# A second, rounding transfer for the high parts of weights in the mixer

## The chip, the cores and the metric

The kernel runs on one core of a Trainium2 chip. The metric is the device time of one launch in microseconds, the median of three runs. The profile shows one execution of the same program.

## What is computed

The reference is two decoder layers on 512 tokens of 1024 channels, all in float32:

```python
for l in range(DEPTH):                       # DEPTH = 2
    x = layer_norm(ALPHA * x + 0.5 * swiglu(x, ffn1_wg[l], ffn1_wu[l], ffn1_wd[l]), ...)
    x = layer_norm(ALPHA * x + token_mixer(x, w_in[l], ...), ...)
    x = layer_norm(ALPHA * x + 0.5 * swiglu(x, ffn2_wg[l], ffn2_wu[l], ffn2_wd[l]), ...)
# token_mixer: x @ w_in gives queries, latents, keys, values, and two gates of 1024 channels;
#   o_m = 8 heads of latent attention; o_n = 8 heads of sparse attention (compressed, selected, window)
#   y = sigmoid(gate_m) * (o_m @ w_proj_mla) + sigmoid(gate_n) * (o_n @ w_proj_nsa);  return y @ w_out
```

## The kernel before

**Products.** A float32 product is made of three matmuls in the type fp32r (`mm3`, lines 226 to 229): each operand is split into a high part, which is the value rounded to fp32r, and a low part, which is the value minus the high part. The three are high by high, high by low and low by high.

**The stream of weights.** All weights lie in DRAM in the order of use (`full_plan`), cut into chunks of at most 128x1024 (512 KB). The class `Stream` (from line 241) brings them in. `load` issues one transfer per chunk from SyncE (SP) into a ring of three tiles `raw` (`RAW_RING`). `pump` splits a chunk: ScalarE (ACT) writes the high part (line 301), VectorE (DVE) the low part (`sub_lo`, line 224), both into one tile `hl` of a ring of four (`HI_RING`); a `raw` tile is free again when both have read it, and an `hl` tile when TensorE (PE) has done the last matmul with it. The program calls `pump` in `get` (a chunk is fetched) and in `done` (a chunk is used up); there it splits chunks up to `LOOK` = 2 beyond those fetched. `live` counts the `hl` tiles in use.

**The mixer.** The attention part of a layer is written as a list of some 200 named steps, `SCHEDULE`. `S`, `N`, `T`, `P` with a number are the scores and softmax, the normalising, the transposing and the product with the values of one of 24 attention units. Between them stand steps that use weights: `m4a` to `m7b` and `n0a` to `n7b` (gates of the two branches, a chunk each, half of it in each of two steps), `cw00` to `cw11` (the compression's first matrix, four chunks), `p0` to `p7` (the first branch's output projection, a chunk for every two), `c2` (192 columns). `keys` and `v0` to `v3` hold four chunks each; `v3` releases the last four one after another. `w_proj_nsa` and `w_out` follow behind the list.

**Other transfers of the mixer.** GpSimd (POOL) issues stores and loads of intermediates: `sv` (values, line 998), `sg` (gates, line 729), `gl` (gates back, line 903), `sy` (results, line 897), `ym` and `tn` (lines 1304 and 1305). SP issues `lc` (line 1023, the step `cl1`), which reads back the values that `sv` stored; the transposes of the step `cb1` (`cd`, line 1040) need them.

**What sets the order.** The program runs under a planner that orders the instructions of PE, ACT, DVE and SP by the order of the text and by when it thinks their inputs are ready, on a model of its own. So a conversion may be placed ahead of the step that calls for it, as soon as its `hl` tile is free. POOL is taken out of this (`manual_schedule`): its instructions stand in the order of the text, and each waits for its own inputs with the next ones behind it. Every engine works through its list in order.

Of the kernel before, what the change touches and what calls it, by code (L numbers as in the profile page):

```python
# [12 lines left out]
AF = mybir.ActivationFunctionType  # L13
# [30 lines left out]
PEND_AT = 3  # L44
TAIL = 4
GROUPS = (10, 8)
LOOK_PAIR = 4

PASS, STAY, TAIL_KIND, PAIR_A, PAIR_B, PAIR_C = range(6)

# [29 lines left out]
def stat_chunk(name, l, c0):  # L82
    return [(name, l, k, c0, c0 + 128) for k in range(KB)]


def tok_chunks(l, c0, c1):
    return [[("w_in", l, 2 * c + j, c0, c1) for j in range(2)] for c in range(KB // 2)]


def uq_chunk(l, half):  # L90
    return [("w_uq", l, k, half * 384, half * 384 + 384) for k in range(2)]


def ukv_chunk(l, part):
    return [("w_ukv", l, 0, part * 512, part * 512 + 512)]


def w1_chunk(l, kind, jh):
    return [("cmp_k_w1" if kind == 0 else "cmp_v_w1", l, 8 * jh + j, 0, 128) for j in range(8)]


def w2_chunk(l):
    return [("cmp_k_w2", l, 0, 0, 64), ("cmp_k_w2", l, 0, 0, 64), ("cmp_v_w2", l, 0, 0, 64)]


def proj_chunk(l, name, m):
    return [(name, l, k, c * 128, c * 128 + 128) for c in (m, m + 1) for k in range(4)]


def down_chunk(name, l, dh, i):  # L110
    return [(name, l, 2 * i + j, dh * 512, dh * 512 + 512) for j in range(2)]


def pair_chunk(name, l, p, part):

    k, halves = ((2 * p, (0, 1)), (2 * p + 1, (1,)), (2 * p + 1, (0, 1)))[part]
    return [(name, l, k, dh * 512, dh * 512 + 512) for dh in halves]


def gate_chunk(l, which, m):  # L120
    return stat_chunk("w_in", l, (COL_GM if which == "m" else COL_GN) + m * 128)


def layer_plan(l):


    p = []

    def add(c, kind=PASS):
        p.append((c, kind))  # L130

    def down(name, nkb):
        n = nkb // 2
        for dh in range(2):
            for i in range(n):
                add(down_chunk(name, l, dh, i), TAIL_KIND if dh == 1 and i >= n - TAIL else PASS)

    def tok(c0, c1):
        for c in tok_chunks(l, c0, c1):
            add(c)  # L140

    def ffn(n):
        at = 0
        for g in GROUPS + (0,):
            end = at + g if g else NF
            for fi in range(at, end):
                add(stat_chunk(n + "_wg", l, fi * 128))
                add(stat_chunk(n + "_wu", l, fi * 128))
            pairs = range(at // 2, end // 2)
            at = end  # L150
            if g:
                for j in pairs:
                    add(pair_chunk(n + "_wd", l, j, 0), PAIR_A)
                    add(pair_chunk(n + "_wd", l, j, 1), PAIR_B)
                for j in pairs:
                    add(pair_chunk(n + "_wd", l, j, 2), PAIR_C)
            else:
                for j in pairs:
                    for dh in range(2):
                        add(down_chunk(n + "_wd", l, dh, j), TAIL_KIND)  # L160

    ffn("ffn1")
    for m in range(4):
        add(gate_chunk(l, "m", m))
    tok(COL_A, COL_B)
    tok(COL_B, COL_C)
    add(uq_chunk(l, 0))
    add(uq_chunk(l, 1))
    add(ukv_chunk(l, 0), STAY)
    add(ukv_chunk(l, 1))  # L170
    for n in SCHEDULE:
        if n == "keys":
            tok(COL_C, COL_D)
        elif n == "v0":
            tok(COL_D, COL_GM)
        elif n[0] in "mn" and n[-1] == "a":
            add(gate_chunk(l, n[0], int(n[1])))
        elif n[:2] == "cw":
            add(w1_chunk(l, int(n[2]), int(n[3])))
        elif n == "c2":  # L180
            add(w2_chunk(l))
        elif n[0] == "p" and n[1] in "0246":
            add(proj_chunk(l, "w_proj_mla", int(n[1])))
    for m in range(0, KB, 2):
        add(proj_chunk(l, "w_proj_nsa", m))
    down("w_out", KB)
    ffn("ffn2")
    return p


def full_plan():
    return [c for l in range(L) for c in layer_plan(l)]


def width(chunk):
    return sum(c[4] - c[3] for c in chunk)
# [3 lines left out]
def hybrid_kernel(ctx: ExitStack, tc: tile.TileContext, x, wflat, lnp, rmsg, small, cst, out):  # L200
    nc = tc.nc
# [7 lines left out]
    def slab(name, dt=F32):  # L209
        return slabs.tile([128, 512], dt, tag="slab", name=name)  # L210
# [9 lines left out]
    act = nc.scalar.activation  # L220
    mm = nc.tensor.matmul

    def sub_lo(o, src, hi):
        tt(out=o, in0=src, in1=f(hi), op=ALU.subtract)  # L224
# [6 lines left out]
    class Chunk:  # L231
        def __init__(self, hi, lo, w, both):
            self.hi, self.lo, self.w, self.both = hi, lo, w, both
# [7 lines left out]
    class Stream:  # L241


        def __init__(self):
            self.plan = full_plan()
            self.n_dma = self.n_split = self.n_got = self.live = 0
            self.off = 0
            self.raw = {}
            self.parts = {}
            self.sums = []  # L250

# [3 lines left out]
        def load(self, most=RAW_RING):  # L255
            while self.n_dma < len(self.plan) and self.n_dma < self.n_split + most:
                i = self.n_dma
                n = width(self.plan[i][0])
                t = rings.tile([128, 1024], F32, tag="raw", bufs=RAW_RING, name=f"raw{i}")
                src = wflat[self.off:self.off + 128 * n].rearrange("(p n) -> p n", p=128)  # L260
                step = self.piece(i, n)
                for j in range(0, n, step):
                    nc.sync.dma_start(out=t[:, j:min(n, j + step)], in_=src[:, j:min(n, j + step)])
                self.off += 128 * n
                self.raw[i] = t
                self.n_dma += 1

        def pump(self):
            self.load()
            while self.n_split < self.n_dma:  # L270
                i = self.n_split
                chunk, kind = self.plan[i]
                look = LOOK
                if kind == TAIL_KIND:
                    look = LOOK_TAIL
                elif kind >= PAIR_A:
                    look = LOOK_PAIR
                elif self.n_got and self.plan[self.n_got - 1][1] == TAIL_KIND:
                    look = LOOK_HEAD
                if i >= self.n_got + look or (kind not in (STAY, TAIL_KIND) and self.live >= HI_RING):  # L280
                    break
                n = width(chunk)
                if kind >= PAIR_A:
                    self.pair(i, kind)
                    continue
                if kind != PASS:
                    w = 512
                    hi = [slab(f"whi{i}", F32R) for _ in range(0, n, w)]
                    lo = [slab(f"wlo{i}", F32R) for _ in range(0, n, w)]
                else:  # L290
                    w = 1024
                    t = rings.tile([128, 2, w], F32R, tag="hl", bufs=HI_RING, name=f"hl{i}")
                    hi, lo = [t[:, 0, :]], [t[:, 1, :]]
                    self.live += 1
                r = self.raw.pop(i)
                step = min(w, self.piece(i, n))
                for j in range(0, n, step):
                    e = min(step, n - j)
                    a = j % w
                    h = hi[j // w][:, a:a + e]  # L300
                    act(out=h, in_=r[:, j:j + e], func=AF.Copy)  # L301
                    sub_lo(lo[j // w][:, a:a + e], r[:, j:j + e], h)
                self.parts[i] = Chunk(hi, lo, w, t if kind == PASS else None)
                self.n_split += 1
                self.load()

# [244 lines left out]
    def ffn(l, n, ln_idx, last):  # L551
# [19 lines left out]
        done = 0  # L571
        for g in GROUPS:
            ops = []
# [888 lines left out]
```

## Time and profile before

| what | value |
|---|---|
| median of three runs | 2219.08 us (2218.5 to 2219.31) |
| the profiled execution | 2218.88 us |
| its span, from the first to the last instruction | 2217.1 us |
| granted TensorE clock, mean | 0.999 of 2.4 GHz |
| mixer steps with weights, layer 1 and layer 2 | about 486 to 700 us and 1586 to 1800 us of the span |
| DMA, mean over the span | 118 GB/s |
| transfers issued by POOL | 34.61 MB, 4.4% of the 16 DMA engines' time |

The profile gives the busy time of each engine, by stretch and by line, and for each idle stretch of an engine what ended it. A line such as 224 or 301 belongs to a helper that many places call; the tile's name tells which place it is (`hl` is a streamed weight, `pl` the low part of attention weights). PE is TensorE's matmuls, PEld its weight loads. POOL's DMA instructions are the issue on the engine, and the time to landing runs from there to the last byte's arrival.

### The profile page before, as it was taken

The numbers are of one execution on the slowest core, as the hardware profiler recorded it, in microseconds if no ns is written. First come the engines' busy times: TensorE is split into PE (matmuls) and PEld (weight loads), VectorE is DVE, ScalarE is ACT, GpSimd is POOL, SyncE is SP. The second block draws the span as 40 slices with busy tenths as digits, with TensorE's granted clock in tenths as the row PEclk, the third lists the DMA queues.
The fourth block names the chain that finished last, engine by engine and source line by source line (L and its number), as shares of the span: only waits on it lengthen the run. The fifth ranks groups of instructions, "written<-read, shape, count | busy, mean of one in ns | idle before, by whom it ended". The sixth has DMA issues, their size and how long they took to land. (4 is left out here: it accounts for less than half of the span.)

```text
span 2217.1 us, 29650 instructions
## 1 busy us (share of the span) xinstructions
PE 2195.5 (99%) x11138; PEld 1880.9 (85%) x11138; DVE 1521.7 (69%) x2886; ACT 965.8 (44%) x1810; POOL 102.9 (5%) x166
## 2 busy tenths in 40 slices
PE   9999999999999999999999999999999999999998
PEld 8888889998888888888898888899988889888886
DVE  5585676578887656758655948665788966576586
ACT  3343332469765233334333434314797742343331
POOL 0000001010002000000000000010100010000000
PEclk9999999999999999999999999999999999999999
DMA  5333343344225233424422433433432272333242
GB/s 177 91 122 115 100 146 121 119 137 131 98 84 205 95 105 92 141 86 133 132 73 89 141 102 105 155 115 110 139 130 91 72 247 69 103 110 123 81 138 86
DMA packets 91520, 261.03 MB, mean 118 GB/s; under 512 B 18801, under 2 KB 22001, under 8 KB 91377
## 3 DMA queue, kind: packets, MB, share of 16 engines
q1 hardware_dynamic: 80464, 224.01, 31.6%
q0 software_dynamic: 10624, 34.61, 4.4%
q8 instruction: 87, 1.43, 0.3%
q10 hardware_dynamic: 288, 0.52, 0.1%
q14 instruction: 57, 0.46, 0.1%
HBM read 234.99 MB, written 24.12 MB: 117 GB/s over the span
## 5 line engine op out<-in xcount | busy, mean ns | idle before, releaser
L224 DVE TENSOR_TENSOR hl<-raw,hl 128x1024 fp32r<-128x1024 f32 (+5 forms) x391 | 443.4, 1140 | 208.7 <-ACT hl L301 163.0
L301 ACT ACTIVATE hl<-raw 128x1024 fp32r<-128x1024 f32 (+2 forms) x283 | 288.8, 1022 | 485.0 <-issue 214.2
L227 PE MATMUL gu<-xTh,hl 128*128 128x512 f32 x1280 | 498.0, 389 | 0.0
L228 PE MATMUL gu<-xTl,hl 128*128 128x512 f32 x1280 | 498.0, 389 | 0.0
L229 PE MATMUL gu<-xTh,hl 128*128 128x512 f32 x1280 | 497.9, 389 | 0.0
L227 PEld LDWEIGHTS gu<-xTh,hl 128*128 128x128 f32 x1280 | 240.3, 188 | 49.9
L228 PEld LDWEIGHTS gu<-xTl,hl 128*128 128x128 f32 x1280 | 240.3, 188 | 49.7
L229 PEld LDWEIGHTS gu<-xTh,hl 128*128 128x128 f32 x1280 | 240.3, 188 | 49.7
L556 DVE TENSOR_TENSOR t<-t,gu 128x512 f32<-128x512 f32 x80 | 55.0, 688 | 174.2 <-PE gu L229 174.2
L310 ACT ACTIVATE hl<-raw 128x1024 fp32r<-128x1024 f32 (+1 forms) x108 | 97.4, 916 | 124.3 <-PE gu L229 85.3
L555 DVE SCALAR_TENSOR_TENSOR t<-t,gu 128x512 f32<-128x512 f32 x80 | 54.9, 686 | 140.3 <-ACT t L554 140.3
L554 ACT ACTIVATE t<-gu 128x512 f32<-128x512 f32 x80 | 47.5, 594 | 205.3 <-PE gu L229 205.3
L680 ACT ACTIVATE P<-P,nm 128x384 f32<-128x384 f32 x192 | 105.6, 552 | 39.0 <-DVE nm L678 34.8
L227 PE MATMUL d<-hl,ph_s 128*128 128x512 f32 x288 | 113.0, 392 | 1.1 <-DVE u L530 0.9
L228 PE MATMUL d<-hl,ph_s 128*128 128x512 f32 x288 | 112.1, 389 | 0.0
L229 PE MATMUL d<-hl,pl_s 128*128 128x512 f32 x288 | 112.1, 389 | 0.0
L224 DVE TENSOR_TENSOR pl<-pt,ph 128x512 fp32r<-128x512 f32 x144 | 79.2, 595 | 23.8 <-ACT ph L704 23.3
L426 POOL TENSOR_TENSOR rs<-rs,ct 128x1 f32<-128x1 f32 x24 | 22.3, 930 | 1515.5 <-DVE rs L425 1515.5
L382 ACT ACTIVATE xTh<-xtp 128x512 fp32r<-128x512 f32 x48 | 25.6, 598 | 147.1 <-PE xtp L379 147.1
L678 DVE CUSTOM_DVE_ANT_0 P<-sc,maskw 128x384 f32<-128x384 f32 x192 | 82.8, 485 | 2.3 <-PE sc L672 2.1
L227 PE MATMUL gf<-xTh,hl 128*128 128x512 f32 x192 | 77.2, 402 | 0.0
L229 PE MATMUL gf<-xTh,hl 128*128 128x512 f32 x192 | 75.2, 392 | 0.0
(366 smaller groups left out, 4603.2 us busy)
## 6 DMA issues: line engine op xcount, KB each, us to landing
raw<-in_wflat_dram SPq DMA_DIRECT2D x343, 512.0 KB, 3.5
raw<-in_wflat_dram SPq DMA_DIRECT2D x40, 256.0 KB, 2.6
gb<-in_lnp_dram SPq DMA_DIRECT2D x24, 256.0 KB, 5.7
raw<-in_wflat_dram SPq DMA_DIRECT2D x12, 384.0 KB, 3.1
sy<-gl POOLq DMA_DIRECT2D x16, 256.0 KB, 2.8
xr<-spill SPq DMA_DIRECT2D x16, 256.0 KB, 5.6
ym<-sy POOLq DMA_DIRECT2D x16, 256.0 KB, 6.3
raw<-in_wflat_dram SPq DMA_DIRECT2D x8, 416.0 KB, 4.0
```

Of the source, the lines that this page charges most:

```text
L224: tt(out=o, in0=src, in1=f(hi), op=ALU.subtract)
L227: mm(o, lh, rh, start=start, stop=False)
L228: mm(o, lh, rl, start=False, stop=False)
L229: mm(o, ll, rh, start=False, stop=stop)
L301: act(out=h, in_=r[:, j:j + e], func=AF.Copy)
L310: act(out=hi, in_=r, func=AF.Copy)
L382: act(out=h, in_=bv, func=AF.Copy)
L554: act(out=t, in_=g, func=AF.Tanh, scale=0.5)
L555: stt(out=t, in0=t, scalar=1.0, in1=g, op0=ALU.add, op1=ALU.mult)
L556: tt(out=t, in0=t, in1=u, op=ALU.mult)
L678: nc.vector.tensor_tensor_reduce(out=o, in0=ps[b][:, off:off + n], in1=maskw[:, T - n:T], scale=1.0, scalar=BIG, op0=ALU.add, op1=ALU.min, ...
L680: act(out=o, in_=o, func=AF.Exp, bias=self.nm[:, qb:qb + 1], scale=-1.0, accum_out=self.l[:, qb:qb + 1])
```

## The change

A kind `CAST` is added for 20 chunks of each layer: the gates of the steps `m4a` to `n7a` (12), `cw00` to `cw11` (4) and `p0` to `p6` (4), each 512 KB. For these the high part is no longer written by ACT from `raw`: POOL issues a second transfer of the same bytes of DRAM straight into the high half of the `hl` tile, and the change of type from float32 to fp32r in the transfer rounds them. The transfer into `raw` stays, since DVE forms the low part from `raw` minus the high part as before. `CAST` chunks are split up to `LOOK_CAST` = 3 beyond those fetched, not 2. Nothing changes for `w_in`'s other parts, `w_uq`, `w_ukv`, `c2`, `w_proj_nsa`, `w_out` and the two feed-forward parts.

```diff
+LOOK_CAST = 3
-PASS, STAY, TAIL_KIND, PAIR_A, PAIR_B, PAIR_C = range(6)
+PASS, STAY, TAIL_KIND, PAIR_A, PAIR_B, PAIR_C, CAST = range(7)
...
         elif n[0] in "mn" and n[-1] == "a":
-            add(gate_chunk(l, n[0], int(n[1])))
+            add(gate_chunk(l, n[0], int(n[1])), CAST)
         elif n[:2] == "cw":
-            add(w1_chunk(l, int(n[2]), int(n[3])))
+            add(w1_chunk(l, int(n[2]), int(n[3])), CAST)
...
-            add(proj_chunk(l, "w_proj_mla", int(n[1])))
+            add(proj_chunk(l, "w_proj_mla", int(n[1])), CAST)
...
                 self.raw[i] = t
+                self.src[i] = src
...
+                elif kind == CAST:
+                    look = LOOK_CAST
...
                 r = self.raw.pop(i)
+                if kind == CAST:
+                    nc.gpsimd.dma_start(out=hi[0][:, 0:n], in_=self.src[i])
...
-                    act(out=h, in_=r[:, j:j + e], func=AF.Copy)
+                    if kind != CAST:
+                        act(out=h, in_=r[:, j:j + e], func=AF.Copy)
                     sub_lo(lo[j // w][:, a:a + e], r[:, j:j + e], h)
```

## Rows read from the trace of the kernel before

**Rows 1.** Page, part 1: busy us of each engine, share of span, instructions.

```profile
PE 2195.5 (99%) x11138; PEld 1880.9 (85%) x11138; DVE 1521.7 (69%) x2886; ACT 965.8 (44%) x1810; POOL 102.9 (5%) x166
```

**Rows 2.** Windows: us, length, busy of PE, PEld, DVE, ACT, POOL, clock, DMA share, GB/s.

```profile
486.00:700.00 214.00, 209.74 (x1231) 183.26 (x1231) 171.28 (x479) 163.26 (x413) 21.54 (x39) 1.00 0.37 121
1586.00:1800.00 214.00, 210.11 (x1231) 183.31 (x1230) 171.38 (x478) 163.01 (x412) 21.99 (x40) 1.00 0.37 122
500.00:550.00 50.00, 49.11 (x299) 43.55 (x300) 40.96 (x105) 46.80 (x118) 4.54 (x8) 1.00 0.40 130
550.00:600.00 50.00, 47.82 (x297) 42.19 (x296) 44.04 (x141) 40.06 (x106) 3.81 (x7) 1.00 0.31 106
```

**Rows 3.** Waits of PE in both mixers (first three rows: layer 1).

```profile
PE pm L227 <- DVE pl L224: 1.7, 1, 1.7
PE cd L1040 <- DMA lc<-sv: 1.5, 1, 1.5
PE cs L1217 <- ACT qs L1158: 0.5, 1, 0.5
PE cd L1040 <- DMA lc<-sv: 1.1, 1, 1.1
```

**Rows 4.** Groups by shape, ACT and DVE, 486 to 700: count | busy, mean ns | idle.

```profile
L301 ACT ACTIVATE hl<-raw 128x1024 fp32r<-128x1024 f32 x25 | 26.3, 1056 | 9.5 <-PE pm L229 5.1 <-PE pn L229 4.4
L224 DVE TENSOR_TENSOR hl<-raw,hl 128x1024 fp32r<-128x1024 f32 x25 | 30.4, 1215 | 8.4 <-ACT hl L301 8.4
L690 DVE TENSOR_SCALAR P<-P,l 128x512 f32<-128x512 f32 x21 | 10.1, 480 | 0.0
L690 DVE TENSOR_SCALAR P<-P,l 128x256 f32<-128x256 f32 x21 | 7.4, 351 | 0.0
```

**Rows 5.** Waits of DVE, 486 to 700.

```profile
DVE l L684 <- ACT P L680: 10.8, 11, 2.2
DVE pl L224 <- ACT ph L704: 10.4, 9, 3.0
```

**Rows 6.** Groups of POOL, 486 to 700: the longest and the commonest issues.

```profile
L903 POOL DMA_DIRECT2D gl<-sg0m x8 | 4.5, 567 | 12.2 <-DVE qTl L224 10.5 <-PE pt L698 1.2 <-DVE qst L224 0.3
L998 POOL DMA_DIRECT2D sv<-nv x1 | 0.7, 713 | 9.4 <-ACT gat L997 9.4
```

**Rows 7.** Tiles raw, gl, tn, 486 to 700, in this order: time to landing.

```profile
DMA to landing us min/median/max: 3.2/4.0/6.8
DMA to landing us min/median/max: 2.3/3.0/5.4
DMA to landing us min/median/max: 5.0/6.2/6.8
```

**Rows 8.** Timeline, 580 to 583, PE (first two), then DVE.

```profile
580.32 0.44 PE L698 MATMUL pt<-ident,P 128*128 128x128 f32 x2 [0.46 <-DVE pl L224]
582.45 0.50 PE L227 MATMUL pm<-oh,hl 128*128 128x512 f32 x1 [1.69 <-DVE pl L224]
580.18 0.47 DVE L690 TENSOR_SCALAR P<-P,l 128x512 f32<-128x512 f32 x1
580.58 1.22 DVE L224 TENSOR_TENSOR hl<-raw,hl 128x1024 fp32r<-128x1024 f32 x1
581.71 1.01 DVE L224 TENSOR_TENSOR pl<-pt,ph 128x512 fp32r<-128x512 f32 x2
```

**Rows 9.** Timeline of SP, POOL and PE, 490 to 501.

```profile
490.63 3.48 SPq L263 DMA_DIRECT2D raw<-in_wflat_dram  x3
492.38 0.71 POOL L998 DMA_DIRECT2D sv<-nv  x1 [9.39 <-ACT gat L997]
494.27 4.14 SPq L1023 DMA_DIRECT2D lc<-sv  x4
500.78 0.63 PE L1040 MATMUL cd<-ident,lc 128*128 128x128 f32 x4 [1.47 <-DMA lc<-sv]
```

**Rows 10.** Window 495 to 500, columns as in rows 2.

```profile
495.00:500.00 5.00, 4.30 (x27) 3.48 (x24) 2.35 (x8) 4.92 (x13) 0.00 (x0) 1.00 0.99 299
```

More of the change, by code (lines that the diff above doesn't have):

```diff
@@ L248, in __init__ @@
             self.raw = {}
+            self.src = {}
             self.parts = {}
@@ L275, in pump @@
                     look = LOOK_TAIL
-                elif kind >= PAIR_A:
+                elif PAIR_A <= kind <= PAIR_C:
                     look = LOOK_PAIR
+                elif kind == CAST:
+                    look = LOOK_CAST
                 elif self.n_got and self.plan[self.n_got - 1][1] == TAIL_KIND:
@@ L282, in pump @@
                 n = width(chunk)
-                if kind >= PAIR_A:
+                if PAIR_A <= kind <= PAIR_C:
                     self.pair(i, kind)
                     continue
-                if kind != PASS:
+                if kind in (STAY, TAIL_KIND):
                     w = 512
@@ L300, in pump @@
                     h = hi[j // w][:, a:a + e]
-                    act(out=h, in_=r[:, j:j + e], func=AF.Copy)
+                    if kind != CAST:
+                        act(out=h, in_=r[:, j:j + e], func=AF.Copy)
                     sub_lo(lo[j // w][:, a:a + e], r[:, j:j + e], h)
-                self.parts[i] = Chunk(hi, lo, w, t if kind == PASS else None)
+                self.parts[i] = Chunk(hi, lo, w, t if kind in (PASS, CAST) else None)
                 self.n_split += 1
```

## The prediction

> **What bounds the kernel now.** I read the page's busy shares first: PE is busy for 99% of the span, ACT for 44%, POOL for 5% [rows 1]. So a gain can only come from PE's idle time, and I looked at where that lies within the two stretches that hold the changed chunks. Windows of 214 us each show PE busy for 209.74 and 210.11 us [rows 2]: 4.26 and 3.89 us idle, 8.15 us in all or 0.37% of the run, at a granted clock of 1.00 throughout. That is the ceiling of any gain here, unless PE's own work changed, and the change does not touch it.
>
> The waits of PE say what that idle time is [rows 3]. In layer 1 it is three things: 1.7 us in the step `p1`, put down to DVE's low parts of attention weights (`pl`); 1.5 us in `cb1`, where the transposes wait for the values that SP reads back (`lc`); 0.5 us on ACT's `qs`. Layer 2 has the same list with 1.1 us for `lc`. None of them is a wait for a streamed weight `hl`: the stream is ahead of PE everywhere.
>
> Then the helpers. ACT is the engine that is relieved, and it is crowded in just one part: 46.80 of 50 us busy from 500 to 550, 40.06 in the next 50 us [rows 2]. Yet PE is busy for 49.11 us of the first of these and loses more in the second (47.82), where DVE has 44.04 us of work. So the engine next to PE is DVE, not ACT. DVE is idle for 214 - 171.28 = 42.7 us per layer, and much of this is waiting for ACT: 8.4 us for high parts of weights in `hl` [rows 4], 10.8 and 10.4 us for softmax and for `ph` [rows 5].
>
> **What the change removes.** Per layer 20 ACT copies of 1.056 us [rows 4], 21.1 us. ACT goes from 163.3 to 142 us of 214. On PE's path this is worth at most the wait that names ACT, 0.5 us, and whatever part of DVE's waits for ACT reaches PE through `pl`. I take -0.5 us per layer for the first (bounds -0.5 and 0).
>
> **The gap in `p1`.** The timeline shows it well [rows 8]: PE waits 0.46 us until 580.32 and 1.69 us until 582.45, each time for a PSUM bank that DVE must read out. DVE is not waiting there, it is working: between the normalising at 580.18 and the two `pl` at 581.71 stands one low part of a weight chunk, which holds the line from 580.58 to 581.71, 1.13 us. The changed chunks get their low part when their transfer has landed, so the planner will put this one elsewhere, before or after. If it moves out, 1.13 us of the gap goes; if ACT's relief lets DVE do more beforehand, up to 0.46 + 1.69 = 2.15 us; if another one moves in, 1.2 us are added. I take -0.6, half of the first, as the place is open.
>
> **What it adds: issues on POOL.** 20 per layer. The nearest rows are POOL's present issues, 0.567 us in the common group and 0.713 us at most [rows 6]: 11 to 14 us per layer. POOL has 214 - 21.54 = 192 us idle [rows 2], which hides them; without that cover they would delay POOL's own stores by as much each. A cast also waits on POOL for its `hl` tile, that is, for PE's last matmul with the chunk four before it. Behind it in POOL's line stand gate stores, `sy`, `gl`; the stores cannot start before PE reaches later steps anyway, and `gl` is fetched well ahead of its use. I cost this at 0, at most one landing (6.8 us) if a `gl` came late.
>
> **What it adds: bytes.** 20 x 524,288 bytes = 10.5 MB per layer in 214 us, 49 GB/s beside the present 121 at a DMA share of 0.37 [rows 2]. At the same cost per byte the share becomes 0.52. That is room on average, but not everywhere: from 495 to 500 us the share is 0.99 at 299 GB/s [rows 10], and there lies the chain of the second gap. POOL stores the last values at 492.38, SP has issued three loads of weights from 490.63 and the four `lc` from 494.27, and PE gets the data at 500.78 [rows 9]. With the change, three casts start as `v3` releases its tiles, before the store, and a fourth stands on POOL directly behind it. One cast is 524 KB / 299 GB/s = 1.75 us of that full stretch, so `lc` comes up to 1.75 us later. Against this, the three `raw` loads now wait for low parts that wait for casts, and may fall behind `lc`; then the wait of 1.5 us could vanish. I take +1.0 per layer, nearer to the first end because the fourth cast is sure to stand there.
>
> **What it adds: a wait in DVE's line.** No row shows a transfer that changes type. Its landing is bounded from below by the fastest landing of the same bytes without it, 3.2 us, and from above by the slowest, 6.8 us; the median is 4.0 [rows 7]. POOL's 256 KB loads land in 3.0 us, and in 6.2 when many are queued. I take 4.0. DVE's low part (1.215 us each) waits for it, and behind it wait softmax, normalising and `pl` of the running unit. If the planner expects the landing right, the low part is placed when the data is there and costs nothing; each microsecond that it lands later than planned is one in which DVE stands. Today DVE stands 8.4 us at the same instructions for ACT without PE losing more than the gap above, so I take +0.5 per layer (bounds 0 and 13, worked out below). PE itself has time: three chunks ahead at 214 / 20 = 10.7 us per chunk is 32 us, against 6.8 + 1.2 = 8.0 us.
>
> **The sum.** -0.5 - 0.6 + 0 + 1.0 + 0.5 = +0.4 us per layer, +0.8 in all. The profiled execution took 2218.88 us (span 2217.1 and 1.78 around it), 0.20 below the median of the runs: 2219.08 + 0.8 = 2219.9 us.
>
> **The rivals.** *Slower: casts land late and hold DVE.* Per 50 us there are 50 / 10.7 = 4.7 casts. If each lands t us after its place in DVE's line, the stretch 550 to 600 needs 44.04 + 4.7 t of DVE, which passes 50 at t = 1.3; that is the point from which it decides. The whole mixer passes 214 at t = (214 - 171.28) / 20 = 2.1. At t = 2.1 the dense stretch alone costs 44.04 + 9.9 - 50 = 3.9 us per layer, 7.8 in all: 2227 us. At t = 6.8 - 4.0 = 2.8 the whole mixer costs 171.28 + 56 - 214 = 13.3 per layer, 26.6 in all: 2246 us. For it: landings of up to 6.8 us exist, and the `lc` wait shows the planner early by 1.5 us on a chain of transfers. Against it: no wait of PE for `hl` now, and DVE's waits for ACT shrink at the same time.
>
> *Slower too: DVE keeps GpSimd from writing the transfer's descriptors.* The normalising takes 480 ns for 512 columns and 351 for 256 [rows 4]: 129 ns for the second 256, 0.50 ns per column, against 1215 / 1024 = 1.19 for a low part. So it runs in a faster mode, and four of them stand in a row per unit. If a cast waited for such a row, t would be up to 4 x 0.48 = 1.9, or 44.04 + 4.7 x 1.9 - 50 = 3.0 us per layer, 6 in all: 2226 us. Against it: POOL's issues keep to 0.567 us on average beside a DVE that is busy 80% of the time [rows 2, 6]. The Trainium skill (SBUF - State Buffer, section "SBUF: two separate sides") says that DVE in its two-port mode locks GpSimd out, so that transfers issued there lack descriptors; the issue times do not show it, while the spread of the landing of `gl`, 2.3 to 5.4 us, leaves room for it.
>
> *Faster: DVE's line clears.* The gap in `p1` goes in both layers (2 x 2.15), the wait for `qs` too (2 x 0.5), and `lc` stays as it is: -5.3, 2214 us. For it: 29.6 of DVE's 42.7 us of idle time are waits for an ACT that loses 13% of its work. Against it: DVE is fully at work in the gap itself.
>
> *The high parts come too late for PE*, because POOL cannot issue ahead of the text as ACT's copies could be placed ahead: 1 us for each of 40 casts would give 2259; with 32 us against 8 I hold it for unlikely.
>
> **How the numbers follow.** No change that can be told: 0.50, with 2215 to 2224 as its own range (the measurement tells a change from none at about 0.2%, 4.4 us). Late casts 0.18, descriptors 0.06, late for PE 0.04: together 0.28 slower. DVE's line clears 0.22: faster. The ceiling of 8.15 us puts nothing below 2210.9; I set the low end at 2212, which leaves out 0.04, and the high end at 2231, which takes in the slower cases up to t = 2.4 and leaves out 0.11.
>
> **What would show it.** Right: ACT near 142 us per mixer, POOL with 40 more issues, PE idle 3 to 6 us per mixer, no wait of PE for `hl`; the wait on `lc` between 1.5 and 3 us; that on `pl` shorter than 1.7. Wrong: DVE's low parts of `hl` waiting for DMA by more than 26 us per layer (20 x 1.3), the landing of the casts above 5.3 us in the median, or `lc` late by more than 2 us; on the other side, PE busy for more than 212 of 214 us.

## The result, and the profile after

The changed kernel takes 2253.11 us (median of 4 runs, 2252.15 to 2253.52) against 2219.19 us for the kernel before on the same chip: a ratio of 1.0148, 95% interval 1.0135 to 1.0160. It is slower by some 33 us, and the forecast of 2219.9 us (2212 to 2231) is missed on the slow side.

What the change should do, it does. The page after, part 1 (columns as in [rows 1]):

```profile
PE 2209.1 (98%) x11138; PEld 1888.9 (84%) x11138; DVE 1522.9 (68%) x2886; ACT 929.6 (41%) x1770; POOL 124.6 (6%) x206
```

ACT has 40 instructions and 36 us less, POOL 40 issues and 22 us more, DVE the same 2886 instructions. The loss is in PE, in two parts. Its idle time went from 2217.1 - 2195.5 = 21.6 to 2251.6 - 2209.1 = 42.5 us, +20.9. And the same 11138 matmuls took 13.6 us longer. Together 34.5 us, all of the longer span.

**The idle part.** The waits of PE in layer 1, 486 to 720 us (columns: engine, tile and line, what ended the wait; total, times, longest), to be laid beside [rows 3]:

```profile
PE cd L1048 <- DVE pl L225: 3.1, 1, 3.1
PE pt L706 <- DVE P L698: 2.7, 1, 2.7
PE qsT L1163 <- DVE qst L225: 2.4, 2, 1.2
PE sc L680 <- DVE hs L1088: 1.2, 1, 1.2
PE sc L680 <- DVE qTl L225: 1.1, 1, 1.1
PE pt L706 <- DVE nm L686: 1.0, 1, 1.0
PE pt L706 <- DVE pl L225: 0.8, 1, 0.8
PE gf L228 <- DVE nm L686: 0.6, 1, 0.6
PE sc L680 <- DVE pl L225: 0.5, 1, 0.5
```

The wait on `pm` of [rows 3] is gone. In its place stand these nine rows, and each but the first names a result of VectorE that is not a weight: normalised `P`, `qst`, `hs`, `qTl`, `nm`, `pl`. No row says that PE waits for a streamed chunk. The first row names `pl`, which ended at about the same moment. But the second of the `lc` transfers, issued at 498.48, landed at 503.03, 0.14 us before PE went on; in layer 2, where the row names `lc`, the distance is the same 0.14 us. So it is the `lc` chain, as the timeline from 491 us shows (start, length, engine, line, operation, idle before it; compare [rows 9]):

```profile
491.85 0.73 POOL L1006 DMA_DIRECT2D sv<-nv  x1 [1.16 <-ACT gat L1005]
492.74 4.41 SPq L265 DMA_DIRECT2D raw<-in_wflat_dram  x3
497.32 2.76 SPq L1031 DMA_DIRECT2D lc<-sv  x4
503.17 1.08 PE L1048 MATMUL cd<-ident,lc 128*128 128x128 f32 x4 [3.12 <-DVE pl L225]
```

SyncE's three weight loads, whose raw buffers now come free later, start at 492.74 instead of 490.63 us and still stand ahead of the `lc` loads, which start 3.05 us later than before. In layer 2 the same wait is 4.88 us.

**The slow part.** Windows of the kernel after (columns as in [rows 2]; the clock is the third number from the end):

```profile
500.00:505.00 5.00, 1.88 (x8) 1.67 (x8) 3.67 (x10) 1.80 (x6) 0.00 (x0) 0.81 1.09 303
505.00:510.00 5.00, 5.00 (x33) 4.50 (x32) 1.00 (x2) 3.25 (x9) 0.56 (x1) 0.85 0.23 61
585.00:590.00 5.00, 2.85 (x22) 2.46 (x22) 5.00 (x16) 3.99 (x11) 0.00 (x0) 0.85 0.61 191
590.00:595.00 5.00, 2.27 (x11) 2.11 (x11) 4.64 (x12) 1.76 (x5) 0.00 (x0) 0.50 0.35 108
595.00:600.00 5.00, 5.00 (x17) 3.97 (x16) 3.58 (x10) 2.16 (x6) 0.00 (x0) 0.63 0.00 0
```

[Rows 2] have a granted clock of 1.00 everywhere. Here it falls to 0.50, the 1.2 GHz level, twice in each layer. In layer 1, windows of 0.5 us put this at about 503 to 506.5 us, behind 3.12 us of idle time, and at about 588.5 to 598.5 us. From 595 to 600 the average is still 0.63, although PE is busy all through. The matmuls of the projections into `pm` from 576 us on take 391 ns in the median and 774 at most. Not every wait is followed by a fall: from 540 to 545 and from 570 to 575 PE stands for 1.2 us each, and the clock stays at 1.00, as it does behind the 1.69 us of [rows 8]. Windows of 1 us, with PE's busy time in each times the part of the clock that is missing, give an estimate of 9.7 us for both layers; the other 4 of the 13.6 us lie at a clock of 1.00 and were not traced.

**Where VectorE stands.** Groups and waits of DVE, 486 to 720 us (compare [rows 4, 5]), and the time from issue to landing of the casts in layer 1:

```profile
L225 DVE TENSOR_TENSOR hl<-raw,hl 128x1024 fp32r<-128x1024 f32 x25 | 30.6, 1223 | 21.4 <-DMA hl<-in_wflat_dram 10.4 <-ACT hl L309 4.6 <-PE ksT L1192 3.9
DVE l L692 <- ACT P L688: 10.3, 10, 1.3
DVE pl L225 <- ACT ph L712: 6.7, 6, 1.8
DMA to landing us min/median/max: 3.5/5.0/7.6
```

DVE stands 10.4 us for landings in this layer, 5.6 in the other. That is 0.5 us for a cast in layer 1. It looked like too little for 33 us, and the experiments say why it is not where the time shows.

### The profile page after: what moved, and what is told of

Its sections match the earlier page's. It is cut to its first block, busy times and chain, and to the rows that moved or that the text cites. A ratio compares the mean times of both kernels' runs of the same rounds, so it can differ in the third digit from the quotient of the medians.

```text
span 2251.6 us, 29685 instructions
## 1 busy us (share of the span) xinstructions
PE 2209.1 (98%) x11138; PEld 1888.9 (84%) x11138; DVE 1522.9 (68%) x2886; ACT 929.6 (41%) x1770; POOL 124.6 (6%) x206
## 5 line engine op out<-in xcount | busy, mean ns | idle before, releaser
L309 ACT ACTIVATE hl<-raw 128x1024 fp32r<-128x1024 f32 (+4 forms) x243 | 246.9, 1017 | 482.1 <-issue 213.9
```

## The experiments

All ratios are to the kernel before, run beside them; "+ us" is (ratio - 1) x 2219. The runs are of five chips, so rows are compared by these two columns.

| kernel | us | ratio, 95% interval | + us |
|---|---|---|---|
| look3_only | 2218.40 | 0.9996 (0.9986 to 1.0006) | -1 |
| bytes_only | 2225.66 | 1.0026 (1.0017 to 1.0035) | 6 |
| wait_only | 2243.82 | 1.0109 (1.0094 to 1.0124) | 24 |
| lc_act | 2264.30 | 1.0199 (1.0181 to 1.0216) | 44 |
| look4 | 2261.21 | 1.0179 (1.0161 to 1.0197) | 40 |
| look2 | 2248.74 | 1.0126 (1.0110 to 1.0142) | 28 |
| planned | 2247.13 | 1.0124 (1.0106 to 1.0142) | 28 |
| stores_act | 2252.65 | 1.0136 (1.0114 to 1.0157) | 30 |
| pe_only | 2228.65 | 1.0038 (1.0023 to 1.0053) | 8 |
| dve_only | 2249.15 | 1.0129 (1.0113 to 1.0144) | 29 |
| first4 | 2253.84 | 1.0145 (1.0127 to 1.0163) | 32 |
| low_later | 2240.15 | 1.0092 (1.0077 to 1.0107) | 20 |
| line2_after | 2249.91 | 1.0132 (1.0115 to 1.0149) | 29 |
| line2_before | 2270.30 | 1.0228 (1.0212 to 1.0243) | 51 |
| dve_line | 2254.00 | 1.0157 (1.0140 to 1.0174) | 35 |
| pe_line | 2233.35 | 1.0063 (1.0048 to 1.0078) | 14 |
| mix_cast | 2261.70 | 1.0191 (1.0176 to 1.0206) | 42 |
| mix_rest | 2247.57 | 1.0123 (1.0106 to 1.0140) | 27 |

### The parts of the change, one at a time

`look3_only` keeps ScalarE's copies and only splits three chunks ahead. `bytes_only` is the same with the second transfer sent into a DRAM tile that nobody reads. `wait_only` has no second transfer: GpSimd copies the chunk from the raw buffer.

```diff
-                    nc.gpsimd.dma_start(out=hi[0][:, 0:n], in_=self.src[i])
+                    nc.gpsimd.dma_start(out=spare[:, 0:n], in_=self.src[i])      # bytes_only
+                    nc.gpsimd.tensor_copy(out=hi[0][:, 0:n], in_=r[:, 0:n])      # wait_only
-                    if kind != CAST:
-                        act(out=h, in_=r[:, j:j + e], func=AF.Copy)
+                    act(out=h, in_=r[:, j:j + e], func=AF.Copy)                  # look3_only, bytes_only
```

> The 20 chunks per layer are still split three ahead, but ACT writes their high parts as before and POOL issues no second transfer. Theory W (work stands in line behind transfers that land late) and theory B (the bytes of the second transfer crowd out others): 2217 to 2222 us, PE idle about 4 us per mixer, no drop of the granted clock. Theory L (the third chunk ahead takes DVE and tile slots at the wrong time): above 2235.

> As look3_only, and POOL issues the second transfer of the same bytes with the same change of type, but into a DRAM tile that nobody reads; ACT writes the high parts. So POOL's line and the DMA engines carry the load, and no engine waits for it. Theory W: within 5 us of look3_only, that is 2217 to 2226, with most of that at the step that reads the values back. Theory B: at least two thirds of the 34 us, 2242 to 2253. The writes go to DRAM and not to SBUF, which is the one difference in load.

> As the changed kernel, but POOL makes the high part by a copy from raw instead of a second transfer: the same place in POOL's line in the order of the text, the same engine before DVE, no added bytes and a delay of one copy (some 1 to 2 us) instead of a landing of about 5 us. Theory W, with the landing as the delay: most of the loss goes, 2220 to 2232. If POOL's line itself is the delay (casts stand behind stores that wait): 2240 to 2253. Theory B: 2217 to 2222.

The look costs nothing, but it is not without effect. In `look3_only`, PE's wait on `pm` in layer 1 is gone too, and its idle time is 2216.2 - 2199.0 = 17.2 us instead of 21.6; its work is 3.5 us longer instead. The granted clock falls there, against what was expected, with PE standing for only 0.41 us (windows as above):

```profile
575.00:580.00 5.00, 4.59 (x36) 4.16 (x36) 4.71 (x15) 4.96 (x13) 0.00 (x0) 0.94 0.28 88
580.00:585.00 5.00, 5.00 (x20) 4.03 (x19) 5.00 (x11) 2.04 (x5) 0.00 (x0) 0.72 0.06 23
```

The bytes, which nobody waits for and which leave the order of every other instruction as it was, cost some 6 us; their wait for `lc` is 2.7 and 2.9 us. So four fifths of the loss needs somebody who waits for the copy, as far as writes to DRAM stand for writes to SBUF. `wait_only` fits that (+24), but it missed its expected time and settles less than it was to: GpSimd's copies slowed DVE. Page, part 1, and the normalising group (compare 480 ns in [rows 4]):

```profile
PE 2210.4 (99%) x11138; PEld 1891.9 (84%) x11138; DVE 1545.9 (69%) x2886; ACT 929.3 (41%) x1770; POOL 146.8 (7%) x206
L698 DVE TENSOR_SCALAR P<-P,l 128x512 f32<-128x512 f32 x21 | 12.1, 574 | 0.0
```

### The `lc` chain

`lc_act` lets ScalarE issue the four loads; `first4` gives the four chunks beside the chain back to ScalarE, so that 16 casts a layer stay.

```diff
-                    nc.sync.dma_start(out=tv[:, :, :, u, :],
+                    nc.scalar.dma_start(out=tv[:, :, :, u, :],                   # lc_act
-            add(gate_chunk(l, n[0], int(n[1])), CAST)
+            add(gate_chunk(l, n[0], int(n[1])), PASS if n in FIRST else CAST)    # first4: m4a, m5a, m6a, cw00
```

> The changed kernel with one difference: the loads that read the stored keys and values back are issued by ACT instead of SP, so they no longer stand behind the weight loads that wait for low parts. If the wait in that step is a place in SP's line: the 3.1 and 4.9 us of PE there fall to 1 us or less and the half-clock stretch behind them goes, 2240 to 2245. If it is bandwidth (DMA share above 1 there): 2250 to 2254.

> The first four of the 20 chunks of each layer (m4, m5, m6, cw00, those beside the chain sv, raw loads, lc) go back to ScalarE; 16 casts stay. W with the lc chain as a term of its own (3.2 us of PE idle in the layers together and some 2 to 4 us of slower clock behind it): 2240 to 2249 us. If the chain were the main cause: 2228 to 2236 us. If only the later casts count: 2250 to 2255 us.

Both missed. With `lc_act` the loads start only at 502.6 us in layer 1, between ScalarE's softmax instructions, the waits for `lc` are still 2.9 and 2.8 us, and PE's idle time is 48.4 us instead of 42.5. `first4` does what it was made for: its waits for `lc` are 1.8 and 1.1 us, from 3.1 and 4.9. Yet the time is the same, since its wait for `qst` became 4.7 us where it was 2.4:

```profile
PE qsT L1164 <- DVE qst L226: 4.7, 2, 3.3
PE pt L707 <- DVE P L699: 2.7, 1, 2.7
PE cd L1049 <- DMA lc<-sv: 1.8, 1, 1.8
```

One wait shrank and another grew. VectorE's line has another order in this trace (low parts, `oc` and `pb` stand elsewhere); that this order made the wait for `qst` grow was not shown here.

### Does GpSimd issue the casts too late?

The theory (P) was that a cast is late because GpSimd's line stands in the order of the text, behind stores and loads that wait. `look4` and `look2` change the look, `planned` lets the planner order GpSimd's line, `stores_act` takes the gate stores out of it.

```diff
-LOOK_CAST = 3
+LOOK_CAST = 4                                          # look4; look2 has 2
-    with tc.manual_schedule(engines={mybir.EngineType.Pool}):
+    if True:                                           # planned
-            nc.gpsimd.dma_start(out=sp_g[w, m], in_=t)
+            nc.scalar.dma_start(out=sp_g[w, m], in_=t) # stores_act
```

> The changed kernel with LOOK_CAST = 4: a cast then stands in POOL's line at the end of a chunk, ahead of that chunk's gate store, instead of behind it; the tile it needs is the same one. Theory P (casts are issued late because POOL's line is in the order of the text, and the low parts then fall into DVE's dense stretches): casts start 2 to 4 us earlier, 2235 to 2245 us. Theory Q (the landing of about 5 us and the planner's new order cost the time, wherever the issue stands): 2250 to 2256.

> The changed kernel with LOOK_CAST = 2: each cast stands about one chunk later in POOL's line, though its tile is free at the same time as before. Theory P: the other side of look4, 2262 to 2280 us. Theory Q: 2250 to 2256.

> The changed kernel with POOL's line left to the planner, as the lines of the other engines are: a cast may stand ahead of stores that still wait. SP's line comes out the same as in the changed kernel. Theory P: 2225 to 2240 us. Theory Q: 2250 to 2256.

> The changed kernel with the gate stores (sg) issued by ACT, which makes their data, so that they no longer stand in POOL's line ahead of casts. Theory P: 2235 to 2245 us, a little less than by look4 as ACT takes the issues. Theory Q: 2250 to 2256.

None of the four gains more than 0.3%, and the largest look is the slowest; only `stores_act` lies in a range that was expected, that of Q. But as a test of P most of them failed: in layer 1 the casts of `look4` start 2.2 us later in the median than those of the changed kernel, each on the time of its own span, those of `look2` 1.9 us later and those of `stores_act` 0.4 us earlier. Only `planned` starts them clearly earlier, by 4.3 us, and its ratio of 1.0124 overlaps the changed kernel's 1.0148. So P is not borne out, by one run. VectorE's waits for landings are 22 to 26 us over both layers in all four, against 16.0 in the changed kernel, and yet three of the four are no slower.

### Who pays for the wait?

Both kernels make the second transfer. In `pe_only` it feeds TensorE alone; in `dve_only` it feeds VectorE's subtraction alone. The other reader takes ScalarE's copy; the half of the chunk that the low part is to fill serves as the second place. The diff is that of `pe_only`; in `dve_only` the transfer goes to `lo[0]`, ScalarE writes `hi`, and VectorE subtracts in `lo`.

```diff
                     h = hi[j // w][:, a:a + e]
+                    if kind == CAST:                   # pe_only
+                        h = lo[j // w][:, a:a + e]
-                    if kind != CAST:
-                        act(out=h, in_=r[:, j:j + e], func=AF.Copy)
+                    act(out=h, in_=r[:, j:j + e], func=AF.Copy)
                     sub_lo(lo[j // w][:, a:a + e], r[:, j:j + e], h)
```

> TensorE alone reads what the second transfer brings: ScalarE writes high parts again, but into the half that the low part is to take, and VectorE subtracts there in place, so it waits for ScalarE as before the change. Same transfers, same bytes, same issues by GpSimd. W (VectorE's line stands for late landings): 2223 to 2230 us, as with the bytes alone, and the waits of VectorE for a DMA into hl are gone. V (the high parts reach TensorE too late): 2245 to 2256 us, with waits of PE for DMA hl of 10 us or more in a layer.

> The other half: the second transfer lands in the half of the low part, VectorE subtracts it there in place and so waits for the landing; TensorE reads high parts that ScalarE wrote. W: 2246 to 2258 us, as the changed kernel. V: 2223 to 2232 us.

This parts them cleanly: `pe_only` is 8 us above before, close to the bytes alone, and `dve_only` 29, close to the changed kernel. PE has its high parts in time, as the prediction said; VectorE's dependence on the landing costs some 20 us. The 8 us of `pe_only` go with the `lc` chain, one wait in each layer, and in its mixers the granted clock is below 1.00 only behind these two (502 to 507 and 1605 to 1613 us):

```profile
PE cd L1049 <- DMA lc<-sv: 4.6, 1, 4.6
PE cd L1049 <- DVE pl L225: 4.5, 1, 4.5
```

That is 9.1 us where [rows 3] have 1.5 + 1.1. The second row, of layer 2, names `pl` as above; PE went on 0.14 us behind the landing of an `lc` transfer.

### Standing, or the order of the line?

`low_later` issues the cast at the same place but puts its low part one chunk later, so that the landing has more time; the load that follows into its `raw` tile moves with it.

```diff
+        def lows(self):
+            while self.low and self.low[0][0] < self.n_got + LOOK_LOW:                   # LOOK_LOW = 2
+                i, o, r, h = self.low.pop(0)
+                tc.keep_in_program_order(sub_lo(o, r, h))
+                self.load()
...
+                if kind == CAST:
+                    self.low.append((i, lo[0][:, 0:n], r[:, 0:n], hi[0][:, 0:n]))
...
```

> The cast is issued where it was, three chunks ahead, but VectorE's low part of it is put one chunk later and held behind what stands ahead of it in the program, so that the landing has one chunk's time more. A raw buffer comes free later for it, so the third load ahead starts later. W: 2226 to 2240 us, VectorE's waits for DMA hl under 3 us in a layer. V: 2248 to 2258 us (PE's need of the high part is not moved). If the kept raw buffers decide: above 2256 us.

The best of the kernels in which VectorE reads casts, 2240 us, but at the upper end of what was expected. DVE's waits for landings fell from 10.4 and 5.6 to 3.3 and 3.9 us, but PE's wait for `P` is 3.4 us in each layer, where the changed kernel has 2.7 and 2.8. So most of the time is lost in another way than by standing for a landing. I therefore fixed whole lines, instruction by instruction, by edges that only set the order (the same was done for TensorE):

```diff
+        dve = [i for i in nc.cur_bb.bb.instructions if i.engine == mybir.EngineType.DVE]
+        line = [j for s in LINE for j in range(int(s.split("-")[0]), int(s.split("-")[-1]) + 1)]
+        for a, b in zip(line, line[1:]):
+            tc.add_manual_dep(dve[b], dve[a].name, mybir.DependencyInfo(
+                mybir.DependencyClass.NoSync, mybir.DependencyReason.DATA), reason="line")
```

> As pe_only (VectorE waits for ScalarE's high part, TensorE reads the cast one), but the lines of VectorE and TensorE are fixed, instruction by instruction, to those of the changed kernel; SyncE's and GpSimd's come out the same as there too. So no low part waits for a landing, and each stands where the changed kernel has it. S (standing for the landings costs the time): 2224 to 2234 us. O (the other order of VectorE's line, which the planner made because of the casts, costs it): 2244 to 2254 us. Between, 2235 to 2243 us: both in part.

> The changed kernel's waits (VectorE and TensorE both read the cast high part), but the lines of VectorE and TensorE fixed to those of pe_only, which are those of ScalarE's copies; SyncE's comes out as there; GpSimd's line is left to the planner, as in the run planned. S: 2243 to 2262 us, with VectorE's waits for DMA hl above the 10.4 us that a layer of the changed kernel has. O: 2226 to 2236 us. Between, 2237 to 2242 us: both in part.

In `line2_after` VectorE waits for no cast at all, and its low parts wait 7.4 and 7.5 us for ScalarE in the two layers (486 to 735 and 1586 to 1845 us), where the kernel before has 14.0 and 11.9 in the same stretches. It takes 2249.9 us, and its ratio overlaps that of the changed kernel. Its page and its first waits of PE in layer 1 are almost those of the changed kernel, down to PE's 2209.1 us of work:

```profile
PE 2209.1 (98%) x11138; PEld 1889.1 (84%) x11138; DVE 1523.5 (68%) x2886; ACT 966.3 (43%) x1810; POOL 125.2 (6%) x206
...
PE cd L1142 <- DMA lc<-sv: 3.5, 1, 3.5
PE qsT L1257 <- DVE qst L318: 3.1, 4, 1.4
PE pt L800 <- DVE P L792: 2.7, 1, 2.7
```

So my theory of the casts that hold VectorE (S) falls as the direct cause. But `line2_before` shows that it is what the planner avoided: with the waits kept and the lines of ScalarE's copies, the kernel takes 2270.3 us, above both expected ranges. (GpSimd's line is left to the planner in this run; `planned`, where it is so too, was no slower than the changed kernel.) DVE stands 13.6 and 17.0 us for landings, PE has 48.8 us idle and 2218.4 busy. A line laid for data that are there early is dear when they are late (+42 us over `pe_only`), and a line laid for late data costs half of that (+21) even when the data are early.

### Which line, and what in it

By the fixed lists, at least 148 of VectorE's 2694 listed instructions have to be moved to get from the line of `pe_only` to that of the changed kernel, and 44 of TensorE's 11138 (the expectations speak of 27 moved places of TensorE). `dve_line` has only VectorE's new line, `pe_line` only TensorE's, both without waits for landings. The edit is that of `line2_after` with other lists.

> As line2_after (no low part waits for a landing), but TensorE's line is fixed to that of pe_only, so that of the two fixed lines only VectorE's is the changed kernel's (SyncE's follows it in four places). If VectorE's line alone carries the loss: 2244 to 2256 us. If TensorE's 27 moved places carry it: 2226 to 2234 us. Half and half: 2236 to 2242 us.

> The other half: VectorE's line fixed to that of pe_only, TensorE's to that of the changed kernel. If VectorE's line alone carries the loss: 2226 to 2234 us, as pe_only. If TensorE's 27 moved places carry it: 2244 to 2256 us. Half and half: 2236 to 2242 us.

VectorE's line carries it: 2254.0 against 2233.4 us. (SyncE's line follows VectorE's in four places of `dve_line`; that was not parted from it.) Its low parts moved like this in layer 1 (place of each in VectorE's line, in `pe_only` and in the changed kernel; 17 moved, four shown):

```
low part of        pe_only   changed   later by
hl, first moved        543       545          2
hl, fourth moved       578       588         10
hl, eighth moved       636       654         18
hl, eleventh moved     691       704         13
P, 128x256             711       725         14
```

The last row is not a low part. It is a normalising of 0.35 us that the planner moved along, from place 711 to 725, and PE's wait of 2.68 us is for it. VectorE's timeline, first of the kernel before, where the two last pieces of this `P` stand 0.73 us apart:

```profile
575.52 0.48 DVE L690 TENSOR_SCALAR P<-P,l 128x512 f32<-128x512 f32 x1
575.91 0.22 DVE L224 TENSOR_TENSOR kc<-kc 128x64 fp32r<-128x64 f32 x1
576.05 0.28 DVE L224 TENSOR_TENSOR VCl<-vf,VCh 128x128 fp32r<-128x128 f32 x1
576.25 0.35 DVE L690 TENSOR_SCALAR P<-P,l 128x256 f32<-128x256 f32 x1
```

and of the kernel after, where 5.99 us lie between them, and PE's waits in this stretch:

```profile
586.68 0.48 DVE L698 TENSOR_SCALAR P<-P,l 128x512 f32<-128x512 f32 x1
587.08 0.28 DVE L225 TENSOR_TENSOR VCl<-vf,VCh 128x128 fp32r<-128x128 f32 x1
...
588.14 1.22 DVE L225 TENSOR_TENSOR hl<-raw,hl 128x1024 fp32r<-128x1024 f32 x1
...
589.82 1.61 DVE L225 TENSOR_TENSOR pl<-pt,ph 128x512 fp32r<-128x512 f32 x3
591.35 0.74 DVE L1228 TENSOR_TENSOR pc<-cs,ct 128x256 f32<-128x256 f32 x2
592.01 0.74 DVE L1230 TENSOR_TENSOR pc<-pc,cs 128x256 f32<-128x256 f32 x2
592.67 0.34 DVE L698 TENSOR_SCALAR P<-P,l 128x256 f32<-128x256 f32 x1
```

```profile
585.96 0.44 PE L706 MATMUL pt<-ident,P 128*128 128x128 f32 x2 [1.03 <-DVE nm L686]
590.05 0.34 PE L1163 MATMUL qsT<-idr,qst 128*128 128x128 f32 x1 [1.24 <-DVE qst L225]
593.07 1.33 PE L706 MATMUL pt<-ident,P 128*128 128x128 f32 x5 [2.68 <-DVE P L698]
```

DVE has no idle time from 586.68 to 592.67 but does other things first, a low part of 1.22 us among them, and `P` last. In the 15 us from 585 to 600 PE stands for 4.88 us. The granted clock falls behind the wait of 1.03 us, at about 588.5 us; the waits of 1.24 and 2.68 us come when it is at 0.50 already.

Could one have the late low parts without the rest? `mix_cast` is the changed kernel with its waits, each low part at its late place and all else in `pe_only`'s order; `mix_rest` the reverse, without the waits.

> The changed kernel with its real waits for the landings, TensorE's line fixed to that of pe_only, and VectorE's line put together by hand: each low part at the place that it has in the changed kernel (2 to 18 places later than in pe_only, 17 of 20 in a layer), all other instructions in pe_only's order. If the other instructions, which the planner moved along (a normalising 14 places later, for one), carry the loss: 2226 to 2238 us. If the late places of the low parts themselves carry it: 2246 to 2258 us.

> The reverse, without a wait for a landing (ScalarE's high parts for VectorE, as in dve_line): low parts at the places that they have in pe_only, all other instructions of VectorE in the changed kernel's order, TensorE's line that of pe_only. If the other instructions carry the loss: 2244 to 2256 us. If the low parts' places do: 2226 to 2236 us.

Neither half is free. The moved others alone (`mix_rest`) give 2247.6 us, against 2228.7 for `pe_only` and 2254.0 for `dve_line`, so they carry most of it (GpSimd's line is left to the planner in `mix_rest`). But leaving them in place is no way out: `mix_cast` takes 2261.7 us, above both expected ranges, with two waits that the changed kernel has at 1.1 us or not at all:

```profile
PE sc L773 <- DVE qTl L318: 3.1, 1, 3.1
PE cs L1318 <- DVE kc L318: 1.8, 1, 1.8
```

How much of `mix_cast` is its waits for landings (5.8 us in layer 1) and how much the late places was not separated. No kernel with casts beat the one before.

## Why the prediction was wrong

**The failed step** is the wait in DVE's line: "If the planner expects the landing right, the low part is placed when the data is there and costs nothing." It was priced at +0.5 us per layer. The low part was placed late, other instructions were moved with it, and the placing cost: without a wait for a landing, VectorE's line of the changed kernel costs (1.0157 - 1.0038) x 2219 = 26 us by `dve_line` and `pe_only`, and 21 us with TensorE's line too (`line2_after`), 10 to 13 per layer; standing for landings adds little to that in the changed kernel (2253.1 against 2249.9 in `line2_after`, intervals that overlap). A line of 2886 instructions in which PE waits for some results within a fraction of a microsecond is not a resource with 42.7 us to spare; only idle time at those places counts. The end of my bound, 13 us per layer, held the size by luck: it was worked out from standing for landings.

**The `lc` chain** was priced at +1.0 per layer. The direction and the mechanism (bytes in a full stretch, DMA share 0.99 in [rows 10], 1.03 to 1.09 after) held where SyncE's line does not wait for casts: the `lc` loads of layer 1 land in 6.2 us in the median in `bytes_only` and 6.6 in `pe_only`, against 4.8 before. In layer 1 of the changed kernel they land in 4.5 us but are issued 3.05 us later. In `pe_only` the waits grew by 3.1 and 3.4 us, in the changed kernel by 1.6 and 3.8. The hope that SyncE's raw loads fall behind `lc` was wrong: its line is laid ahead, and they kept their place and took `lc` with them.

**The clock** was not in the sum. [Rows 2] show 1.00 everywhere, and I read it as a constant; it is not one. 13.6 of the 34.5 us are PE's longer work, an estimated 9.7 of them at a granted clock below 1.00. Idle time alone does not settle when it falls: it fell in `look3_only` with PE standing for 0.41 us in 5, and did not behind 1.69 us in the kernel before. What makes it fall stays open here.

**The gap in `p1`**, -0.6: the wait on `pm` went, as hoped, but the look did that, as `look3_only` shows with ScalarE's copies kept; its shorter idle time came with as much longer work, and was worth nothing. In the changed kernel waits came at other places. (The prediction's list of three waits in layer 1 also left out the 0.46 us that it uses in `p1`.) **ACT's relief**, -0.5: the wait for `qs` is still 0.5 us in both layers, so it was worth nothing. **POOL's issues** at 0: right as far as shown: 566 ns each (567 in [rows 6]), 22 us in all, and `pe_only`, which has all of them, stays within 8 us of the kernel before. **PE's high parts in time**: right, shown by `pe_only`.

**The rivals.** Late casts had the right engine and the right sign, but its measure was wrong: it asked for a mean of 1.3 us per cast, or 26 us of standing per layer, and 10.4 and 5.6 were measured. An average over a stretch asks whether VectorE has the time; the question was what stands in front of the few results that PE takes next. The median landing of 5.0 us in layer 1 is also below my sign of 5.3. *Descriptors lock*: not shown; issues stayed at 566 ns beside a busy DVE, but whether a part of the 5.0 us of landing is such a wait was not tested. The reverse was seen in `wait_only`, where GpSimd's own copies made a 512-column normalising 574 ns instead of 480 and DVE 23 us busier. The Trainium skill (SBUF - State Buffer, section "SBUF: two separate sides") says that the pair of ports that DVE and GpSimd share is locked by one instruction at a time. `wait_only` is in line with this, by its 574 against 480 ns, but does not tell a lock from a sharing.

## What to carry to other kernels

Moving work off an engine that does not bound changes when its result is ready, and with it the order that a planner gives the engine behind it; price that order, by what stands ahead of the results that the bounding engine takes next, not by the idle share of the engine. To tell bytes, waits and order apart, let each reader take the new data alone, and then fix the lines of one kernel in the other. And where TensorE runs at its full clock all through, expect a change that makes it stand to cost more than the idle time: here 20.9 us of it came with 13.6 us of longer work. This is no fixed price: against the kernel before, `wait_only` has 14.9 us of longer work for 7.8 us of idle time, and `lc_act` 12.2 for 26.8.

## What was not expected of the hardware

The granted clock fell to 0.50 behind a wait of PE of 1.03 us and stayed there for some 10 us, the last 5 of them with PE busy (588.5 to 598.5 us of the changed kernel); in `look3_only` it fell with hardly a wait. A transfer of 512 KB that changes its type landed in 4.7 us in the median (40 of them), against 3.5 for the plain one from SyncE (343); in layer 1 it was 5.0 against 4.2. The issuing engine differs too, so the change of type is not shown to be the reason. And 40 GpSimd copies, 44 us of work, made DVE 1545.9 - 1522.9 = 23 us busier, although none of DVE's instructions changed.
